# Feed-forward weight sums by accumulating transfers instead of VectorE, with other slots for the token factors

## The chip, the cores and the metric

The kernel runs on one core of a Trainium2 chip. Its time is the device time of one execution in microseconds, and lower is better. A core has TensorE (matrix products into PSUM), VectorE, ScalarE and GpSimd (elementwise work in SBUF, the first two also from PSUM), and SyncE, which here issues most of the DMA transfers. Each engine works through its own queue in order.

## The reference

One inference step of a two-layer decoder trunk for a prompt of 512 tokens and a sample group of 8 x 4 tokens; D_MODEL is 1024. Layer 0 mixes by Mamba-2 SSD heads and sliding-window attention, layer 1 by a forgetting attention over paged caches. Each layer then has cross-attention into 256 memory tokens and a feed-forward part; that part holds most of what is changed:

```python
def swiglu(xn, w_in, w_out):
    g, u = jnp.split(xn @ w_in, 2, axis=-1)
    return (jax.nn.silu(g) * u) @ w_out

for l in range(DEPTH):
    ...  # mixing: layer 0 even_split / ssm / swa, layer 1 odd_split / fox
    xp = xp + cross_attn(rms_norm(xp, norm_xa[l]), mk, mv, w_xq[l], w_xo[l])
    xs = xs + cross_attn(rms_norm(xs, norm_xa[l]), cache_mem_k[l], cache_mem_v[l], w_xq[l], w_xo[l])
    ...
    xp = xp + swiglu(rms_norm(xp, norm_ffn[l]), w_ffn_in[l], w_ffn_out[l])
    xs = xs + swiglu(rms_norm(xs, norm_ffn[l]), w_ffn_in[l], w_ffn_out[l])
```

All 544 tokens (512 prompt, 32 sample) go through the products together. The hidden width is 2816, 22 blocks of 128 for g and u each. All data are float32.

## The kernel before

**Order.** The program is written in one order, but a scheduler places each engine's instructions by a simulated timeline, subject to data dependencies, the number of buffers of each tile, and a few order-only edges (`after`). It also packs the tiles into SBUF by their lifetimes, so a tile may reuse the bytes of one that is done.

**Precision.** A float32 product is made of three passes: each operand is split into a rounded high part (a ScalarE cast) and a remainder (a VectorE subtraction), and TensorE adds high·high, high·low and low·high. So each weight block costs one transfer, one cast and one subtraction before it can be used.

**Slots.** `H` is a pool of 13 equal slots of 128 x 2176 float32. Tokens x (2 slots), their high and low parts (4), hidden blocks, attention tiles and token factors all come from it. `wpiece` streams other weights through `raw` (2 buffers), `wh` and `wl` (3 each).

**The feed-forward stage** (`ffn`, called once per layer). The first 3 of the 22 hidden blocks are computed by `plain`, 8 chunks of 128 deep and three passes each, for g and u, in two halves of the tokens. For the other 19 blocks the product of one 2 x 2 block matrix (weights) by another (tokens) is made with seven products instead of eight. `operands` makes the seven token factors b11, b21, b22, t1 to t4 once per stage: VectorE first writes the normalised tokens `xn` (2 slots of H), GpSimd forms differences and a sum in place (L1424, L1429), and each factor goes into a slot of H as cast and remainder (L1415, L1419, or L1417 when its sign changes). `factors` makes the seven weight factors of a hidden block: SyncE loads `raw` (tag `fr`, two buffers, 1 MB, four quarters; L1440), and `split` writes high and low parts (L1450, L1451) into `fh` and `fl` (three buffers each, two factors in one) or into `f1` (two buffers, a22 alone). The four sums s1 to s4 are formed in place in `raw` by VectorE (L1457, L1458, L1460):

```python
        split(("a11", "a12"), raw[:, 2:4])
        split(("a22",), raw[:, 0:1])
        nc.vector.tensor_tensor(raw[:, 0:2], raw[:, 0:3:2], raw[:, 1:2].to_broadcast([P, 2, 512]), ALU.add)
        nc.vector.tensor_tensor(raw[:, 2], raw[:, 2], raw[:, 0], ALU.add)
        split(("s1", "s2"), raw[:, 0:3:2])
        nc.vector.tensor_tensor(raw[:, 3], raw[:, 3], raw[:, 2], ALU.add)
        split(("s3", "s4"), raw[:, 1:4:2])
```

The seven products (`product`, L1467, 12 matmuls each) of block n are made in the order a11, a12, s1, s2 (`begin`, `second`, `third`), and after the next block's a11 s3, then after its a12 a22 and s4 (`fourth`, `last`). a11, s2, s3 and a22 add up in one PSUM bank R, which is copied out between them (to S0, S1, S2: L1540, L1553, L1557; the last through the SiLU into SG, L1564); s1 and s4 add up in R2. GpSimd then multiplies the two halves of the block (L1569), and the result is split into hidden slots. Between the products, `more` puts pieces of the output projection of a finished group of hidden blocks (`outer`, matmuls at L135, weights by `pair`, L1507 and L1508, evacuation L1520).

**The mixing layers.** `even` and `odd` project tokens to V (with dt or the forget gate) by two weight pieces of 4 x 272 columns from `wpiece`; `stack_q` makes a stacked query tile `QS`; `fox_sample` keeps a small tile `ncs`.

Of the kernel before, what the change touches and what calls it, by code (L numbers as in the profile page):

```python
# [19 lines left out]
P = 128  # L20
# [82 lines left out]
class Net:  # L103
# [37 lines left out]
    def wpiece(self, src, kt, w):  # L141
        nc = self.nc
        n = kt * w
        raw = self.wp.tile([P, 1088], F32, tag="raw", bufs=2, name=self.nm("raw"))
        d = nc.sync.dma_start(raw[:, 0:n], src)
# [5 lines left out]
        nc.scalar.copy(hi[:, 0:n], raw[:, 0:n])  # L151
        nc.vector.tensor_tensor(lo[:, 0:n], raw[:, 0:n], hi[:, 0:n].bitcast(F32), ALU.subtract)  # L152
# [292 lines left out]

    def stack_q(self, pool, q, m, tok):

        nc = self.nc
        Q = pool.tile([P, 1088], F32R, tag="QS", bufs=2, name=self.nm("QS"))[:, 0:1024].rearrange("p (r i t) -> p r i t", r=2, i=4)
        for r in range(2):  # L450
            a, b = slice(64 * r, 64 * r + 64), slice(64 - 64 * r, 128 - 64 * r)
            src = q.half(m)[a, :, tok]
            nc.scalar.copy(Q[a, r], src)
            nc.vector.tensor_tensor(Q[b, r], src, Q[a, r].bitcast(F32), ALU.subtract)
        return Q


    def swa_prompt(self, q, K2, V, m):
        nc = self.nc
        for c in range(4):  # L460
            nk = 1 if c == 0 else 2
            W, k0 = 128 * nk, 128 * max(c - 1, 0)
            tok = slice(128 * c, 128 * c + 128)
            Q = self.stack_q(self.sw, q, m, tok)
            PT = self.H("PT")[:, 0:2048].rearrange("p (k r i t) -> p k r i t", k=2, r=2, i=4)
# [122 lines left out]
    def even(self, st, nxt, fill):  # L588
        nc, tc, I, O = self.nc, self.tc, self.I, self.O
        with ExitStack() as es:  # L590
# [9 lines left out]

            wv = [self.wpiece(I["we_v"][i], 4, 272) for i in range(2)]
            nc.gpsimd.memset(dt, 0.0)
# [359 lines left out]
    def odd(self, st, nxt, fill):  # L962
        nc, tc, I, O = self.nc, self.tc, self.I, self.O
        with ExitStack() as es:
# [52 lines left out]
            with tc.tile_pool(name="fox", bufs=1) as fx:  # L1017
                self.pvs = []
# [18 lines left out]
                smp = self.fox_sample(q, kTs, Qb, V, lf, fx, S, sel)  # L1037
# [12 lines left out]
                for c in range(2):  # L1050
                    o, N = CH[c]
                    for j in range(8):
                        last = self.split(oh, ol, q[j][:, o:o + N], j, o, N)
                self.x_load(self.xd, last)
                self.cross_keys(1, last)
                st2 = nxt()
                self.linear(self.pieces(I["wo_d"], KD), range(8), KD, oh, ol, self.x_evac(st2), tail=2, lead=3)
                self.hold = self.whold = None
        return st2

    def fox_prompt(self, q, K2, V, ncum, oh16, fx, m, c, at=(), smp=None):
        nc = self.nc
        W = 128 * (c + 1)
        tok = slice(128 * c, 128 * c + 128)
        Q = self.stack_q(fx, q, m, tok)
        PT = [self.H("PT")[:, 0:2048].rearrange("p (k r i t) -> p k r i t", k=2, r=2, i=4) for _ in range(c // 2 + 1)]
        for r in range(2):
            for i in range(4):
# [9 lines left out]
                nc.vector.tensor_reduce(nm, sc[:, 0:W], AX.X, ALU.max, negate=True)  # L1078
                pr = fx.tile([P, 512], F32, tag="P", bufs=3, name=self.nm("pr"))
                nc.scalar.activation(pr[:, 0:W], sc[:, 0:W], AF.Exp, bias=nm, accum_out=den)  # L1080
                nc.vector.reciprocal(rec, den)
# [57 lines left out]

    def fox_sample(self, q, kTs, Qb, V, lf, fx, S, sel):  # L1140

        nc, I = self.nc, self.I
        c = self.cst
        ncs = fx.tile([32, 16, 4], F32, name="ncs")
        tp = self.psum("tp", [P, 16])
# [290 lines left out]
    def factors(self, src, fp, prev):  # L1436
# [19 lines left out]

        nc.vector.tensor_tensor(raw[:, 0:2], raw[:, 0:3:2], raw[:, 1:2].to_broadcast([P, 2, 512]), ALU.add)  # L1457
        nc.vector.tensor_tensor(raw[:, 2], raw[:, 2], raw[:, 0], ALU.add)  # L1458
        split(("s1", "s2"), raw[:, 0:3:2])
        nc.vector.tensor_tensor(raw[:, 3], raw[:, 3], raw[:, 2], ALU.add)  # L1460
        split(("s3", "s4"), raw[:, 1:4:2])
# [7 lines left out]
    def ffn(self, l, st, nxt):  # L1469
        nc, tc, I = self.nc, self.tc, self.I  # L1470
        with tc.tile_pool(name=f"ffn{l}", bufs=1) as fp:
            t = fp.tile([P, 10 * HT], F32, name="ft")
            part = lambda a, n: t[:, HT * a:HT * (a + n)]
            U, SG, S0, S1, S2, G1 = (part(0, 2), part(2, 2)), part(4, 2), part(6, 1), part(7, 1), part(8, 1), part(9, 1)
            hh, hl = {}, {}
# [8 lines left out]
            def plain(n):  # L1484
                hidden(n)
                wu, wg = (self.wpiece(I["wfi0"][l, 2 * n + r], KD, 128) for r in range(2))
                for c in (0, 1):
# [7 lines left out]
                    g, s = U[n % 2][:, o:o + N], SG[:, o:o + N]  # L1495
                    nc.vector.tensor_tensor(g, pg[:, 0:N], rb, ALU.mult)  # L1496
# [39 lines left out]
            def begin(n):  # L1536
                w = self.factors(I["wfi1"][l, n - FLEAD], fp, ready if n > FLEAD else gate)
                R = self.psum("tr", [P, HT])
                self.product(R, w["a11"], X["b11"], True)
                nc.scalar.copy(S0, R)  # L1540
                return {"n": n, "w": w, "R": R, "u": U[n % 2]}

            def second(p):
                R3 = self.psum("pv", [P, HT])
                self.product(R3, p["w"]["a12"], X["b21"], True)
                nc.vector.tensor_tensor(p["u"][:, 0:HT], R3, S0, ALU.add)

            def third(p, k):
# [3 lines left out]
                self.product(p["R"], p["w"]["s2"], X["t2"], False)  # L1552
                nc.scalar.copy(S1, p["R"])  # L1553

            def fourth(p):
                self.product(p["R"], p["w"]["s3"], X["t3"], False)
                nc.scalar.copy(S2, p["R"])  # L1557
                nc.vector.tensor_tensor(G1, p["R2"], S2, ALU.add)
                nc.scalar.activation(SG[:, HT:NT], G1, AF.Silu, scale=-1.0)

            def last(p, k):
                n = p["n"]
                self.product(p["R"], p["w"]["a22"], X["t4"], False)
                nc.scalar.activation(SG[:, 0:HT], p["R"], AF.Silu, scale=-1.0)  # L1564
                more(k)
                self.product(p["R2"], p["w"]["s4"], X["b22"], False)
                self.last = nc.vector.tensor_tensor(p["u"][:, HT:NT], p["R2"], S1, ALU.add)  # L1567
                hidden(n)
                nc.gpsimd.tensor_tensor(p["u"], p["u"], SG, ALU.mult)  # L1569
                self.split({n: hh[n][:, n % 4]}, {n: hl[n][:, n % 4]}, p["u"], n, 0, NT)  # L1570
                group(n)
# [167 lines left out]
```

## Time and profile before

| | us |
|---|---|
| median of 3 runs | 1732.09 (1731.93 to 1732.36) |
| the profiled execution's own time | 1733.22 |
| span of the profile | 1731.4 |
| TensorE busy | 1666.6 (96%) |
| VectorE busy | 1200.5 (69%) |
| ScalarE busy | 776.9 (45%) |
| GpSimd busy | 429.4 (25%) |

The profiled execution is one of its own, not one of the three timed runs. PE is TensorE, PEld its weight loads, DVE VectorE, ACT ScalarE, POOL GpSimd, SP SyncE. L1457 is line 1457 of the kernel before. A group's row names line, engine, operation, output <- inputs and shape. Rows of the order in time give start, length, engine, line and operation, and in square brackets how long the engine had been idle and what ended that. Times are from the span's start. TensorE's matmuls overlap, so a matmul of 288 ns follows the one before it after about 126 ns.

### The profile page before, as it was taken

Reading aid. Unit: us, or ns where it says so; the run is one execution under the profiler, and the core shown is the slowest. Engines: PE = TensorE matmul, PEld = TensorE weight load, DVE = VectorE, ACT = ScalarE, POOL = GpSimd, SP = SyncE. Lnnn points to the kernel's source line nnn. Section 1 sums busy time; section 2 is a strip of 40 time slices with the busy share of each in tenths; the row PEclk is TensorE's granted clock in tenths of the full one; section 3 lists DMA queues with packets and bytes.
Section 4 is the critical chain, followed back from the end, with each engine's and each line's share of the span. In section 5 each row is a group of like instructions: output and inputs, shape, how many; then the busy total and the mean of one; then the engine's idle time right before and its main releaser. Section 6 shows DMA issues by size and latency. Waiting matters only on the chain.

```text
span 1731.4 us, 32174 instructions
## 1 busy us (share of the span) xinstructions
PE 1666.6 (96%) x12824; PEld 1531.3 (88%) x12824; DVE 1200.5 (69%) x2142; ACT 776.9 (45%) x1575; POOL 429.4 (25%) x550
## 2 busy tenths in 40 slices
PE   6999999989999989999999999889999899999997
PEld 6988899866997989999999997556898899999997
DVE  6667679867866897777766567335577887777753
ACT  4345435344545454444435345325446354444443
POOL 5022323566422511111113013012222501111112
PEclk9999999989999999999999999899999999999999
DMA  4211423127533142222214423444442142323212
GB/s 157 90 50 50 131 93 129 44 94 253 182 98 135 62 146 86 97 98 86 98 40 135 149 62 113 159 171 151 166 143 91 65 148 92 107 78 110 86 47 80
DMA packets 57106, 189.24 MB, mean 109 GB/s; under 512 B 6044, under 2 KB 16060, under 8 KB 49084
## 3 DMA queue, kind: packets, MB, share of 16 engines
q1 hardware_dynamic: 55268, 184.83, 31.9%
q8 instruction: 101, 1.65, 0.4%
q10 hardware_dynamic: 1608, 1.83, 0.4%
q0 software_dynamic: 80, 0.52, 0.1%
q14 instruction: 49, 0.40, 0.1%
HBM read 172.22 MB, written 14.95 MB: 108 GB/s over the span
## 4 chain that ended last, share of the span: by engine, by line
PE 84%; DVE 7%; DMA 3%; ACT 2%; issue 1%; POOL 1%; SPq 1%; DVEq 0%; ACTq 0%; POOLq 0%
PE ps L135 59%; PE ps L1467 23%; PE ps L138 3%; DMA kv<-fox_kv 1%; DVE wl L152 1%; DMA raw<-we_x 1%; DVE fl L1451 1%; DVE xn L1409 1%; DVE xl L228 1%; SPq L1158 0%; DMA raw<-wfo 0%; POOL ft L1498 0%; DMA hb<-state 0%; DVE fr L1457 0%; DVE xs L853 0%
## 5 line engine op out<-in xcount | busy, mean ns | idle before, releaser
L1467 PE MATMUL ps<-xf,fh 128*128 128x272 f32 x1824 | 355.3, 291 | 11.4 <-DVE ft L1496 3.7
L135 PE MATMUL ps<-xh,wh 128*128 128x288 f32 (+1 forms) x1088 | 319.3, 295 | 8.8 <-ACT wh L151 7.9
L135 PE MATMUL ps<-xl,wh 128*128 128x288 f32 (+1 forms) x1088 | 319.5, 295 | 1.2 <-DVE xl L228 1.0
L135 PE MATMUL ps<-xh,wl 128*128 128x288 f32 (+1 forms) x1088 | 317.9, 293 | 1.9 <-DVE wl L152 1.9
L1467 PEld LDWEIGHTS ps<-xf,fh 128*128 128x128 f32 x1824 | 290.1, 190 | 13.6 <-ACT xf L1415 6.8
L1467 PE MATMUL ps<-xf,fl 128*128 128x272 f32 x912 | 258.2, 292 | 0.0
L135 PEld LDWEIGHTS ps<-xh,wh 128*128 128x128 f32 x1088 | 206.4, 190 | 12.6 <-ACT wh L151 7.9
L135 PEld LDWEIGHTS ps<-xl,wh 128*128 128x128 f32 x1088 | 206.3, 190 | 7.1 <-issue 4.9
L1569 POOL TENSOR_TENSOR ft<-ft 128x544 f32<-128x544 f32 x38 | 78.9, 2076 | 527.7 <-DVE ft L1567 512.7
L135 PEld LDWEIGHTS ps<-xh,wl 128*128 128x128 f32 x1088 | 206.5, 190 | 3.3 <-DVE wl L152 2.2
L151 ACT CAST wh<-raw 128x1024 fp32r<-128x1024 f32 (+2 forms) x128 | 130.9, 1023 | 173.8 <-PE ps L135 98.8
L1451 DVE TENSOR_TENSOR fl<-fr,fh 128x1024 fp32r<-128x1024 f32 x114 | 173.7, 1525 | 23.8 <-ACT fh L1450 23.6
L152 DVE TENSOR_TENSOR wl<-raw,wh 128x1024 fp32r<-128x1024 f32 (+2 forms) x128 | 160.7, 1256 | 30.4 <-ACT wh L151 15.2
L1467 PEld LDWEIGHTS ps<-xf,fl 128*128 128x128 f32 x912 | 170.8, 190 | 0.0
L1450 ACT CAST fh<-fr 128x1024 fp32r<-128x1024 f32 x114 | 119.8, 1053 | 94.0 <-DVE fr L1458 51.8
L135 PE MATMUL ps<-hl,oh 128*128 128x256 f32 (+1 forms) x512 | 147.4, 289 | 0.0
L135 PE MATMUL ps<-hh,ol 128*128 128x256 f32 (+1 forms) x512 | 147.1, 288 | 0.0
L135 PE MATMUL ps<-hh,oh 128*128 128x256 f32 (+1 forms) x512 | 146.2, 288 | 0.0
L237 POOL TENSOR_TENSOR room<-room,sq 128x256 f32<-128x256 f32 (+1 forms) x96 | 84.9, 886 | 184.7 <-ACT sq L236 182.7
L135 PEld LDWEIGHTS ps<-hl,oh 128*128 128x128 f32 x512 | 96.5, 188 | 0.0
L135 PEld LDWEIGHTS ps<-hh,oh 128*128 128x128 f32 x512 | 96.3, 189 | 0.0
L135 PEld LDWEIGHTS ps<-hh,ol 128*128 128x128 f32 x512 | 96.3, 188 | 0.0
(425 smaller groups left out, 3783.6 us busy)
## 6 DMA issues: line engine op xcount, KB each, us to landing
fr<-wfi SPq DMA_DIRECT2D x38, 1024.0 KB
or<-wfo SPq DMA_DIRECT2D x32, 512.0 KB
kv<-fox_kv SPq DMA_DIRECT2D x64, 256.0 KB
raw<-wo_e SPq DMA_DIRECT2D x16, 512.0 KB
xk<-mem_k SPq DMA_DIRECT2D x8, 1024.0 KB
xv<-mem_v SPq DMA_DIRECT2D x8, 1024.0 KB
raw<-we_x SPq DMA_DIRECT2D x12, 512.0 KB
raw<-wfi SPq DMA_DIRECT2D x12, 512.0 KB
```

Of the source, the lines that this page charges most:

```text
L135: self.nc.tensor.matmul(out, lhsT, rhs, start=start, stop=stop)
L138: self.nc.tensor.transpose(out, in_, self.ident[0:k, 0:k])
L151: nc.scalar.copy(hi[:, 0:n], raw[:, 0:n])
L152: nc.vector.tensor_tensor(lo[:, 0:n], raw[:, 0:n], hi[:, 0:n].bitcast(F32), ALU.subtract)
L228: return nc.vector.scalar_tensor_tensor(ll, src, g, hh.bitcast(F32), ALU.mult, ALU.subtract)
L237: nc.gpsimd.tensor_tensor(acc, acc, sq[:, 0:N], ALU.add)
L1409: nc.vector.scalar_tensor_tensor(xn[k], self.x[k], self.par[:, st["g"] + k:st["g"] + k + 1], st["b"], ALU.mult, ALU.mult)
L1450: nc.scalar.copy(hi, t)
L1451: nc.vector.tensor_tensor(lo, t, hi.bitcast(F32), ALU.subtract)
L1467: self.nc.tensor.matmul(ps, w[a][:, k], x[:, b, k], start=start and k == 0 and i == 0, stop=k == 3 and i == 2, skip_group_check=True)
L1569: nc.gpsimd.tensor_tensor(p["u"], p["u"], SG, ALU.mult)
```

## The change

The three VectorE additions that make the weight sums become three transfers issued by GpSimd, which add their source to what stands in the destination. The first reads two quarters of the block from DRAM once more and adds them to the first two quarters in SBUF; the second and third go from SBUF to SBUF. `xn` gets two buffers of its own in the stage's pool instead of two slots of H. The stage's work tile `ft` shrinks from 10 x 272 to 4 x 544 columns: S0, S1, S2 and G1 go, their values stand in the final places U and G, and G has two copies where SG had one. The streaming buffers shrink from 1088 to 1024 columns; the V weights of both mixing layers, which are wider, go through `vpieces` and three slots of H. `QS` shrinks in the same way, and `ncs` moves into an unused part of the tile of `odd`.

```diff
     def wpiece(self, src, kt, w):
...
-        raw = self.wp.tile([P, 1088], F32, tag="raw", bufs=2, name=self.nm("raw"))
+        raw = self.wp.tile([P, 1024], F32, tag="raw", bufs=2, name=self.nm("raw"))
...
-        hi = self.wp.tile([P, 1088], F32R, tag="wh", bufs=3, name=self.nm("wh"))
-        lo = self.wp.tile([P, 1088], F32R, tag="wl", bufs=3, name=self.nm("wl"))
+        hi = self.wp.tile([P, 1024], F32R, tag="wh", bufs=3, name=self.nm("wh"))
+        lo = self.wp.tile([P, 1024], F32R, tag="wl", bufs=3, name=self.nm("wl"))
...
+    def vpieces(self, src):
+
+        nc = self.nc
+        raw, hi, lo = self.H("vr"), self.H("vh", F32R), self.H("vl", F32R)
+        out = []
+        for i in range(2):
+            s = slice(1088 * i, 1088 * i + 1088)
+            nc.sync.dma_start(raw[:, s], src[i])
+            nc.scalar.copy(hi[:, s], raw[:, s])
+            nc.vector.tensor_tensor(lo[:, s], raw[:, s], hi[:, s].bitcast(F32), ALU.subtract)
+            out.append([t[:, s].rearrange("p (k w) -> p k w", w=272) for t in (hi, lo)])
+        return out
...
-            wv = [self.wpiece(I["we_v"][i], 4, 272) for i in range(2)]
+            wv = self.vpieces(I["we_v"])
...
+            ncs = t[0:32, 2016:2080].rearrange("p (h t) -> p h t", h=16)
             xh, xl = st["h"], st["l"]
-            wv = [self.wpiece(I["wd_v"][i], 4, 272) for i in range(2)]
+            wv = self.vpieces(I["wd_v"])
...
     def operands(self, st, fp):
...
         xn = Big(self, "xn")
+        xn.h = [fp.tile([P, 4 * NT], F32, tag="xn", bufs=2, name=self.nm("xn")).rearrange("p (k t) -> p k t", k=4) for _ in range(2)]
...
     def factors(self, src, fp, prev):
...
-        nc.vector.tensor_tensor(raw[:, 0:2], raw[:, 0:3:2], raw[:, 1:2].to_broadcast([P, 2, 512]), ALU.add)
-        nc.vector.tensor_tensor(raw[:, 2], raw[:, 2], raw[:, 0], ALU.add)
+        add = lambda out, in_: nc.gpsimd.dma_start(out, in_, accum_op=ALU.add)
+        add(raw[:, 0:2], src.rearrange("p (a w) -> p a w", a=4)[:, 1:3])
+        add(raw[:, 2], raw[:, 0])
         split(("s1", "s2"), raw[:, 0:3:2])
-        nc.vector.tensor_tensor(raw[:, 3], raw[:, 3], raw[:, 2], ALU.add)
+        add(raw[:, 3], raw[:, 2])
         split(("s3", "s4"), raw[:, 1:4:2])
...
     def ffn(self, l, st, nxt):
...
-            t = fp.tile([P, 10 * HT], F32, name="ft")
-            part = lambda a, n: t[:, HT * a:HT * (a + n)]
-            U, SG, S0, S1, S2, G1 = (part(0, 2), part(2, 2)), part(4, 2), part(6, 1), part(7, 1), part(8, 1), part(9, 1)
+            t = fp.tile([P, 4 * NT], F32, name="ft")
+            U, G = ([t[:, NT * i:NT * i + NT] for i in r] for r in ((0, 1), (2, 3)))
...
-                nc.scalar.copy(S0, R)
-                return {"n": n, "w": w, "R": R, "u": U[n % 2]}
+                nc.scalar.copy(U[n % 2][:, 0:HT], R)
+                return {"n": n, "w": w, "R": R, "u": U[n % 2], "g": G[n % 2]}
...
-                nc.scalar.copy(S2, p["R"])
-                nc.vector.tensor_tensor(G1, p["R2"], S2, ALU.add)
-                nc.scalar.activation(SG[:, HT:NT], G1, AF.Silu, scale=-1.0)
+                g = p["g"][:, HT:NT]
+                nc.scalar.copy(g, p["R"])
+                nc.vector.tensor_tensor(g, p["R2"], g, ALU.add)
+                nc.scalar.activation(g, g, AF.Silu, scale=-1.0)
...
-                self.last = nc.vector.tensor_tensor(p["u"][:, HT:NT], p["R2"], S1, ALU.add)
+                self.last = nc.vector.tensor_tensor(p["u"][:, HT:NT], p["R2"], p["u"][:, HT:NT], ALU.add)
                 hidden(n)
-                nc.gpsimd.tensor_tensor(p["u"], p["u"], SG, ALU.mult)
+                nc.gpsimd.tensor_tensor(p["u"], p["u"], p["g"], ALU.mult)
```

More of the change, by code (lines that the diff above doesn't have):

```diff
@@ L444, in stack_k, with stack_q @@
         return kh, kl
-    def stack_q(self, pool, q, m, tok):
+    def stack_q(self, Q, q, m, tok):
         nc = self.nc
-        Q = pool.tile([P, 1088], F32R, tag="QS", bufs=2, name=self.nm("QS"))[:, 0:1024].rearrange("p (r i t) -> p r i t", r=2, i=4)
+        Q = Q.rearrange("p (r i t) -> p r i t", r=2, i=4)
         for r in range(2):
@@ L463, in swa_prompt @@
             tok = slice(128 * c, 128 * c + 128)
-            Q = self.stack_q(self.sw, q, m, tok)
+            Q = self.stack_q(self.sw.tile([P, 1024], F32R, tag="QS", bufs=2, name=self.nm("QS")), q, m, tok)
             PT = self.H("PT")[:, 0:2048].rearrange("p (k r i t) -> p k r i t", k=2, r=2, i=4)
@@ L1017, in odd @@
             with tc.tile_pool(name="fox", bufs=1) as fx:
-                self.pvs = []
+                self.pvs, self.heads = [], 0
                 K2 = self.stack_k(kT)
@@ L1036, in odd @@
                 next(f)
-                smp = self.fox_sample(q, kTs, Qb, V, lf, fx, S, sel)
+                smp = self.fox_sample(q, kTs, Qb, ncs, V, lf, fx, S, sel)
                 heads = 0
@@ L1064, in fox_prompt @@
         tok = slice(128 * c, 128 * c + 128)
-        Q = self.stack_q(fx, q, m, tok)
+        Q = self.stack_q(fx.tile([P, 1024], F32R, tag="QS", bufs=2, name=self.nm("QS"))[:, 0:1024], q, m, tok)
         PT = [self.H("PT")[:, 0:2048].rearrange("p (k r i t) -> p k r i t", k=2, r=2, i=4) for _ in range(c // 2 + 1)]
@@ L1138, in fox_bias, with fox_sample @@
         return S, sel.rearrange("p a t -> p (a t)")
-    def fox_sample(self, q, kTs, Qb, V, lf, fx, S, sel):
+    def fox_sample(self, q, kTs, Qb, ncs, V, lf, fx, S, sel):
         nc, I = self.nc, self.I
         c = self.cst
-        ncs = fx.tile([32, 16, 4], F32, name="ncs")
         tp = self.psum("tp", [P, 16])
@@ L1545, in second @@
                 self.product(R3, p["w"]["a12"], X["b21"], True)
-                nc.vector.tensor_tensor(p["u"][:, 0:HT], R3, S0, ALU.add)
+                nc.vector.tensor_tensor(p["u"][:, 0:HT], R3, p["u"][:, 0:HT], ALU.add)
             def third(p, k):
```

7 lines of the change are left out of this document (4 added, 3 removed).

## The prediction

> **What bounds the kernel now.** I read the table of busy time first, then windows, then the chain that ended last for single stretches, then the order in time of VectorE, ScalarE and GpSimd there.
>
> ```profile
> span 1731.4 us, 32174 instructions
> PE 1666.6 (96%) x12824; PEld 1531.3 (88%) x12824; DVE 1200.5 (69%) x2142; ACT 776.9 (45%) x1575; POOL 429.4 (25%) x550
> 600.00:650.00 50.00, 44.74 (x328) 43.86 (x327) 46.42 (x54) 24.69 (x37) 13.87 (x6) 0.93 0.36 127
> 640.00:890.00 250.00, 250.00 (x1989) 250.00 (x1989) 183.88 (x242) 106.26 (x164) 32.90 (x15) 1.00 0.27 91
> 1350.00:1400.00 50.00, 44.92 (x336) 44.01 (x335) 48.42 (x52) 24.60 (x36) 22.20 (x10) 0.93 0.27 105
> 1400.00:1650.00 250.00, 250.00 (x1989) 250.00 (x1988) 185.44 (x242) 106.31 (x165) 32.34 (x16) 1.00 0.29 96
> ```
>
> A window row gives its length, then busy time of TensorE, weight loads, VectorE, ScalarE and GpSimd, the granted clock, the DMA share and GB/s. The two long rows are the feed-forward stages, where all that the title names happens: TensorE is busy 250.00 of 250 us at clock 1.00. VectorE has 183.88 of 250, so 26% of its time is free, and time taken from it there is worth nothing by itself. The two short rows are the starts of these stages. TensorE stands still for 5.26 and 5.08 us, and VectorE is nearly full (46.42 and 48.42 of 50). Only these 10.3 us are to be won in the feed-forward stages.
>
> **The sums.** In before they are three VectorE instructions per hidden block:
>
> ```profile
> L1457 DVE TENSOR_TENSOR fr<-fr x38: 1212/1216/3200, 604.1 to 1664.3; 128x1024 f32<-128x1024 f32 x38
> L1458 DVE TENSOR_TENSOR fr<-fr x38: 677/679/1521, 607.6 to 1667.8; 128x512 f32<-128x512 f32 x38
> L1460 DVE TENSOR_TENSOR fr<-fr x38: 675/679/694, 608.5 to 1669.1; 128x512 f32<-128x512 f32 x38
> ```
>
> By the medians 38 x (1.216 + 0.679 + 0.679) = 97.8 us leave VectorE. In the full stretches this is nothing on the path. In exchange come 38 x 3 transfers on GpSimd's queue of 512, 256 and 256 KB, in series: the second reads what the first wrote, the third what the second wrote. So the question is how late the weights s1 may be. One block in the steady stretch, by the chain (start, length, what), then VectorE, ScalarE, GpSimd, and one row of TensorE a block later:
>
> ```profile
> 658.48 4.54 PE ps L1467 x36
> 671.40 1.51 PE ps L1467 x12
> 675.10 4.54 PE ps L1467 x36
> 661.84 0.69 DVE L1451 TENSOR_TENSOR f<-fr,f 128x512 fp32r<-128x512 f32 x1 [1.16 <-ACT f L1450]
> 669.08 1.22 DVE L1451 TENSOR_TENSOR fl<-fr,fh 128x1024 fp32r<-128x1024 f32 x1 [0.23 <-ACT fh L1450]
> 671.62 1.23 DVE L1451 TENSOR_TENSOR fl<-fr,fh 128x1024 fp32r<-128x1024 f32 x1 [0.49 <-ACT fh L1450]
> 660.90 0.40 ACT L1564 ACTIVATE ft<-ps 128x272 f32<-128x272 f32 x1 [1.48 <-PE ps L1467]
> 661.20 0.61 ACT L1450 CAST f<-fr 128x512 fp32r<-128x512 f32 x1
> 667.99 1.06 ACT L1450 CAST fh<-fr 128x1024 fp32r<-128x1024 f32 x1 [2.08 <-DVE fr L1458]
> 668.95 0.37 ACT L1553 COPY ft<-ps 128x272 f32<-128x272 f32 x1
> 663.05 2.17 POOL L1569 TENSOR_TENSOR ft<-ft 128x544 f32<-128x544 f32 x1 [13.79 <-DVE ft L1567]
> 692.45 1.68 PE L1467 MATMUL ps<-xf,f 128*128 128x272 f32 x12
> ```
>
> A block lasts 675.10 - 658.48 = 16.62 us. The first transfer overwrites the quarter that the split of a22 reads, so it can start when that split ends, 661.84 + 0.69 = 662.53. The split itself starts as soon as TensorE lets go of a22 two blocks back (660.90), since f1 has two buffers, so this point can't move forward. The other end: after s3 (12 matmuls from 671.40) and a run of the output projection comes a group of 36 from 675.10. A block later the a22 product (the row with f) starts 0.7 us after the group's start (691.7), so some matmuls of s1 or of s4 stand ahead of it. If s1 is first in the group, it is wanted at 675.10; if last, at 679.64 - 1.51 = 678.1. Before it stand the ScalarE cast and VectorE's remainder, 1.06 + 1.22 = 2.3 us. So the first two transfers have 675.1 - 2.3 - 662.5 = 10.3 us, or 13.3.
>
> What do they take? No accumulating transfer stands in before. The nearest rows:
>
> ```profile
> L1103 POOL DMA_INDIRECT lg<-fox_logf,pg x1: 1134/1134/1134, 984.0 to 984.0; - x1
> L1101 ACTq DMA_DIRECT2D pg<-page_col x1: 529/529/529, 980.0 to 980.0; - x1
>   DMA pg<-page_col: 3.4, 1
> DMA to landing us min/median/max: 6.2/6.2/6.2
> q0 software_dynamic: 80, 0.52, 0.1%
> 579.08 0.33 SPq L145 DMA_DIRECT2D raw<-wfi  x1
> 582.68 1.05 ACT L151 CAST wh<-raw 128x1024 fp32r<-128x1024 f32 x1 [1.89 <-DMA raw<-wfi]
> ```
>
> The gather of 0.52 MB is the only transfer that GpSimd issues; it holds that engine 1.13 us and lands after 6.2. A plain load of 512 KB from SyncE's queue goes from issue (579.08) to use (582.68) in 3.6. One of 64 numbers, issued by ScalarE, kept GpSimd waiting 3.4. For the first transfer (512 KB) the ends are 3.6 and 12.4 (the gather twice, since an addition reads both operands); I take 6.2, the row with its size and queue. For the second and third (256 KB) the ends are 3.4 and 6.2; I take 5.1, halfway between the 4.0 of that smallest one (from its issue at 980.0 to 984.0) and 6.2. The first two: 11.3 (ends 7.0 and 18.6).
>
> The Trainium skill, DMA: Bandwidth & Descriptors, section "Anatomy of one DMA — SWDGE (gpsimd) path", gives 2.0 us plus bytes over 436 GB/s. By that, as an estimate, they would take 3.2 and 2.6, together 5.8, and be hidden at either place of s1; the 6.2 of the gather, against 3.2 by that rule, speaks for more.
>
> There is one more thing on GpSimd's queue: the product L1569, 663.05 to 665.22. If it goes ahead of the first transfer, this is issued 2.7 us later. So four corners, missing us per block: s1 first and GpSimd free 11.3 - 10.3 = 1.0; s1 first and behind L1569 3.7; s1 last and free none; s1 last and behind 11.3 + 2.7 - 13.3 = 0.7. The order is made anew by the scheduler, so I take the lower of the two middle corners, 0.7, for (19 - 2) x 2 = 34 steady blocks: **+24 us**. Missing time isn't made up, since TensorE has no free time in a block.
>
> Behind the waiting instructions: on ScalarE the cast for s1 and s2 stands just ahead of L1553, which must empty a bank before s3 adds to it at 671.40. If the cast stays there, its room is 671.4 - 0.4 - 1.1 - 662.5 = 7.4 us, not 10.3 (a rival below). On GpSimd L1569 may wait for a landing, and behind it the split of the hidden block; this is hidden unless a group of hidden blocks ends. The third transfer and the splits of s3 and s4: 662.5 + 11.3 + 0.7 + 5.1 + 2.3 = 681.9, wanted a block after 671.40, at 688.0: hidden by 6 us. The load buffer comes free then, 9 us later than now (671.62 + 1.23); its next load is wanted two blocks after 661.20, at 694.4, and 1 MB at twice 3.6 us lands at 689: hidden by 5. Transfers grow by 38 MB on 189; the share of 0.27 to 0.29 stays far from 1, but the later load now falls beside the next first transfer (upper end).
>
> **The start of each stage.** The token factors:
>
> ```profile
> 597.30 3.56 DVE L1451 TENSOR_TENSOR fl<-fr,fh 128x1024 fp32r<-128x1024 f32 x1
> 600.78 3.05 DVE L1451 TENSOR_TENSOR f<-fr,f 128x512 fp32r<-128x512 f32 x1
> 604.12 3.20 DVE L1457 TENSOR_TENSOR fr<-fr 128x1024 f32<-128x1024 f32 x1
> 609.41 2.89 DVE L1451 TENSOR_TENSOR fl<-fr,fh 128x1024 fp32r<-128x1024 f32 x2 [0.19 <-ACT fh L1450]
> 612.93 1.28 DVE L1419 TENSOR_TENSOR xf<-xn,xf 128x1088 fp32r<-128x1088 f32 x1
> 610.53 2.11 ACT L1415 ACTIVATE xf<-xn 128x1088 fp32r<-128x1088 f32 x2
> 603.36 2.88 POOL L1424 TENSOR_TENSOR xn<-xn,xn 128x1088 f32<-128x1088 f32 x1
> PE ps L1467 <- ACT xf L1415: 2.6, 1, 2.6
> PE ps L1467 <- DVE xf L1419: 2.2, 1, 2.2
> PE ps L1467 <- DVE ft L1496: 3.7, 1, 3.7
> ```
>
> TensorE waits 4.8 us for t1, whose cast starts at 610.53 although GpSimd's differences are done at 606.24: t1 needs one of 13 slots H, all taken until the last plain block lets go of its tokens. Taking xn out of H gives two slots sooner, and the sums' 3.20 + 2 x 0.68 = 4.6 us leave VectorE, for whose late evacuation L1496 the second stage waits 3.7 us. That alone would take away the whole stall, 10.3 us over both stages. But here the split of a22 ends at 603.83, the weights s1 then follow 11.3 + 2.3 us later, at 617.4, or at 613.9 if that split goes ahead of the 3.56 us one; t1's wait ended at 612.93 + 1.28 = 614.2. One stall takes the other's place: I take 0, between -5.2 (a whole stall of a stage gone) and +3.2 (617.4) for each.
>
> **The rest**, each at nothing. Buffers of 1024 instead of 1088, ncs inside another tile, and U and G in place of S0, S1, S2, SG: the same instructions and sizes, and in the long stretches TensorE waits for none of these tiles (250.00 of 250). In both mixing layers V's weights take three H slots instead of the streaming buffers: the same loads, casts and remainders. Their bounds:
>
> ```profile
> PE ps L135 <- ACT wh L151: 8.3, 3, 7.9
> PE ps L135 <- DVE wl L152: 1.9, 1, 1.9
> ```
>
> An earlier load could save the 1.9; two 544 KB loads ahead of others at the kernel's beginning could cost two times 3.6. I keep 0.
>
> **Sum.** 24 + 0 + 0 on the profiled execution, 1733.2 (span 1731.4 and 1.8 around it), gives 1757; the median of the runs is 1.1 lower, so **1756**.
>
> **Rivals.** *Hidden after all* (faster): the first two transfers take under 10.3 us with s1 first, or under 13.3 with s1 last, so no steady block waits, and the starts lose part or all of 10.3 us: 1722 to 1728. For it: both middle corners miss by at most 1.0, and TensorE has fillers to put ahead. It decides at one number, the landing of the second transfer at 672.8 in the block shown. The skill's rule above would lead here. Chance 0.33. *It does nothing*: hidden, and the start's stall only changes its name: within 0.2% (3.5 us, about what a measurement of this kernel can tell from no change). Chance 0.13. *Far dearer*: the cast holds up L1553 (11.3 - 7.4 = 3.9 us per block, 34 x 3.9 = 133, 1864), or the transfers take their upper 18.6 us (8.3 x 34 = 282, 2013). Against the second: the DMA share is low (0.27); for it: an addition has two operands to read. Chance 0.10. The skill, Collectives: The Full Stack, section "The bandwidth ceiling: the fold count and why AG ≠ RS ≠ AR", states that an add in the DMA engines halves the rate through its two source reads; no run so far shows it here. *The forecast*, 0.1 to 2 us missing per steady block: 1736 to 1800, chance 0.44.
>
> The range reaches from the faster rival's 1722 to 1803 (2 us per block and 3 per start over the forecast's base); it leaves out the far dearer case and a little beside it. The forecast's own range is 1736 to 1800. Faster 0.33, same 0.13, slower 0.44 + 0.10 = 0.54.
>
> **What would show it.** Right: windows in the long stretches with TensorE under 250 of 250 and VectorE down by 2.6 us per block; ScalarE's cast for s1 and s2 waiting for a transfer into fr; TensorE waiting for fh there; 11 us from the split of a22 to the second landing. The start: t1's cast before 606, and a wait for fh in its place. Wrong: 250.00 of 250 again (hidden), or a wait for a copy of the banks, L1553 (the dearer case).

## The result, and the profile after

The changed kernel takes 1896.43 us (median of 4 runs, 1888.76 to 1903.93), against 1732.01 (1730.58 to 1732.36): a ratio of 1.0951, 95% interval 1.0901 to 1.1. That is 164.4 us slower, 140 above the forecast and beyond the range. The profiled execution took 1888.76. From its page (busy time, a DMA queue with packets, MB and share, and two groups of transfers with their median landing):

```profile
span 1887.0 us, 32221 instructions
PE 1721.2 (91%) x12824; PEld 1575.7 (84%) x12824; DVE 1096.6 (58%) x2028; ACT 768.0 (41%) x1575; POOL 512.0 (27%) x664
...
q0 software_dynamic: 16496, 40.38, 12.5%
...
fr<-wfi POOLq DMA_DIRECT2D x38, 512.0 KB, 6.8
fr<-fr POOLq DMA_DIRECT2D x76, 256.0 KB, 3.3
```

VectorE lost 103.9 us of work. The first transfer lands a little later than the prediction sized it, the second and third sooner: 6.8 and 3.3 us against 6.2 and 5.1. The windows of the two starts and the two long stretches:

```profile
600.00:650.00 50.00, 37.18 (x240) 35.57 (x239) 32.83 (x31) 18.09 (x28) 19.34 (x14) 0.83 0.50 134
640.00:890.00 250.00, 221.81 (x1598) 218.62 (x1599) 118.35 (x163) 88.01 (x139) 52.95 (x51) 0.91 0.54 132
1440.00:1490.00 50.00, 40.87 (x290) 39.56 (x290) 38.31 (x38) 20.26 (x31) 22.91 (x14) 0.93 0.45 116
1490.00:1740.00 250.00, 217.96 (x1617) 215.41 (x1616) 113.72 (x162) 85.46 (x136) 55.70 (x50) 0.94 0.54 133
```

TensorE starts 1598 matmuls in 250 us where before it started 1989. Measured from the first matmul of `product` to the last, a feed-forward stage takes 383.8 and 378.0 us, against 310.3 and 309.7. That is 141.8 of the 155.6 us by which the span grew; 4.6 lie ahead of the first stage, 8.5 between the stages, 0.7 behind. A block takes 19.8 us (mean distance of its first transfers) in place of 16.62. Who waits (us in total, times, longest):

```profile
PE ps L1483 <- ACT ft L1573: 65.7, 25, 5.6
PE ps L1483 <- ACT fh L1465: 27.1, 12, 5.4
PE ps L1483 <- DVE fl L1466: 8.7, 5, 3.1
ACT fh L1465 <- DMA fr<-fr: 264.5, 73, 7.9
POOL fr L1472 <- DVE f L1466: 288.5, 38, 9.7
```

L1483 is the product, L1465 and L1466 the split, L1472 the transfers, L1573 the copy S2, L1580 the SiLU behind a22. TensorE waits mostly for a small copy, S2, and that copy is late because ScalarE stands in front of it waiting for a transfer: in 29 of the 38 blocks S2's copy starts directly behind a cast that has waited for one. The chain of work over two rounds, then ScalarE's order in the first of them:

```profile
726.73 6.31 DMA fr<-wfi
...
733.58 3.30 DMA fr<-fr
...
736.95 1.05 ACT fh L1465
...
740.77 1.52 PE ps L1483 x12
...
742.32 0.40 ACT ft L1580
742.72 0.52 ACT f L1465
...
743.26 0.70 DVE f L1466
...
744.24 8.78 DMA fr<-wfi
...
757.13 3.27 DMA fr<-fr
...
760.43 1.04 ACT fh L1465
761.47 0.29 ACT ft L1573
...
766.86 5.92 DMA fr<-wfi
```

```profile
736.95 1.04 ACT L1465 CAST fh<-fr 128x1024 fp32r<-128x1024 f32 x1 [3.44 <-DMA fr<-fr]
737.90 0.38 ACT L1573 COPY ft<-ps 128x272 f32<-128x272 f32 x1
740.50 1.05 ACT L1465 CAST fh<-fr 128x1024 fp32r<-128x1024 f32 x1 [2.23 <-DMA fr<-fr]
...
742.32 0.40 ACT L1580 ACTIVATE ft<-ps 128x272 f32<-128x272 f32 x1 [0.43 <-PE ps L1483]
742.61 0.61 ACT L1465 CAST f<-fr 128x512 fp32r<-128x512 f32 x1
```

The chain bites its own tail. The split of a22 releases the first transfer (744.24); the transfers release the cast of s1 and s2, or that of s3 and s4; behind this cast on ScalarE stands S2's copy of the block before; this copy releases TensorE's a22 product; that product lets go of one of the two buffers of `f1`, and so the next a22 split (742.72) can run and releases the next first transfer. From 726.73 to 744.24 the loop takes 17.5 us (the first and second transfer in it), from 744.24 to the next first transfer, at 766.86, 22.6 (all three). Before, the same loop held 2.6 us of VectorE's sums and had slack; now it holds 10 to 16 us of landings and is longer than the 16.6 us that TensorE needs for a block.

### The profile page after: what moved, and what is told of

It is laid out like the page before. It is cut to its first block, busy times and chain, and to the rows that moved or that the text cites. A ratio compares the mean times of both kernels' runs of the same rounds, so it can differ in the third digit from the quotient of the medians.

```text
span 1887.0 us, 32221 instructions
## 1 busy us (share of the span) xinstructions
PE 1721.2 (91%) x12824; PEld 1575.7 (84%) x12824; DVE 1096.6 (58%) x2028; ACT 768.0 (41%) x1575; POOL 512.0 (27%) x664
## 3 DMA queue, kind: packets, MB, share of 16 engines
q0 software_dynamic: 16496, 40.38, 12.5%
## 4 chain that ended last, share of the span: by engine, by line
PE 50%; DMA 22%; issue 10%; DVE 9%; ACT 5%; POOL 3%; SPq 1%; DVEq 0%; POOLq 0%; ACTq 0%
PE ps L135 42%; DMA fr<-wfi 12%; DMA fr<-fr 6%; PE ps L1483 5%; PE ps L138 3%; ACT fh L1465 2%; POOL fr L1472 1%; DVE f L1466 1%; DVE xl L241 1%; DMA kv<-fox_kv 1%; DVE wl L152 1%; DVE fl L1466 1%; POOL room L412 1%; DMA raw<-we_x 1%; SPq L1172 1%
## 5 line engine op out<-in xcount | busy, mean ns | idle before, releaser
L1483 PE MATMUL ps<-xf,fh 128*128 128x272 f32 x1824 | 370.6, 301 | 31.9 <-ACT fh L1465 27.1
L1483 PEld LDWEIGHTS ps<-xf,fh 128*128 128x128 f32 x1824 | 306.0, 201 | 35.5 <-ACT fh L1465 29.9
L1466 DVE TENSOR_TENSOR fl<-fr,fh 128x1024 fp32r<-128x1024 f32 x114 | 160.8, 1413 | 287.4 <-ACT fh L1465 287.4
L1483 PE MATMUL ps<-xf,fl 128*128 128x272 f32 x912 | 270.6, 299 | 8.7 <-DVE fl L1466 8.7
L1465 ACT CAST fh<-fr 128x1024 fp32r<-128x1024 f32 x114 | 119.1, 1048 | 276.6 <-DMA fr<-fr 264.5
L1483 PEld LDWEIGHTS ps<-xf,fl 128*128 128x128 f32 x912 | 180.1, 199 | 10.0 <-DVE fl L1466 10.0
L151 ACT CAST wh<-raw 128x1024 fp32r<-128x1024 f32 (+1 forms) x124 | 126.0, 1019 | 130.9 <-PE ps L135 83.1
L152 DVE TENSOR_TENSOR wl<-raw,wh 128x1024 fp32r<-128x1024 f32 (+1 forms) x124 | 157.0, 1267 | 25.4 <-PE ps L135 17.5
L1483 PE MATMUL ps<-xf,f 128*128 128x272 f32 x456 | 87.3, 356 | 65.7 <-ACT ft L1573 65.7
L1472 POOL DMA_DIRECT2D fr<-fr x76 | 66.3, 872 | 275.6 <-DMA fr<-wfi 150.0
L1483 PEld LDWEIGHTS ps<-xf,f 128*128 128x128 f32 x456 | 78.9, 247 | 71.6 <-ACT ft L1573 71.6
L1472 POOL DMA_DIRECT2D fr<-wfi x38 | 33.2, 875 | 288.5 <-DVE f L1466 288.5
```

What stands on the lines that cost most here:

```text
L1465: nc.scalar.copy(hi, t)
L1466: nc.vector.tensor_tensor(lo, t, hi.bitcast(F32), ALU.subtract)
L1472: add = lambda out, in_: nc.gpsimd.dma_start(out, in_, accum_op=ALU.add)
L1483: self.nc.tensor.matmul(ps, w[a][:, k], x[:, b, k], start=start and k == 0 and i == 0, stop=k == 3 and i == 2, skip_group_check=True)
```

## The experiments

Each kernel's time is beside a kernel before on the same chip (medians 1730.9 to 1732.0). A stage length is, as above, the time from the first to the last matmul of `product`.

**The slots alone.** VectorE's three sums put back into the changed kernel:

```diff
-        add = lambda out, in_: nc.gpsimd.dma_start(out, in_, accum_op=ALU.add)
-        add(raw[:, 0:2], src.rearrange("p (a w) -> p a w", a=4)[:, 1:3])
-        add(raw[:, 2], raw[:, 0])
+        nc.vector.tensor_tensor(raw[:, 0:2], raw[:, 0:3:2], raw[:, 1:2].to_broadcast([P, 2, 512]), ALU.add)
+        nc.vector.tensor_tensor(raw[:, 2], raw[:, 2], raw[:, 0], ALU.add)
...
-        add(raw[:, 3], raw[:, 2])
+        nc.vector.tensor_tensor(raw[:, 3], raw[:, 3], raw[:, 2], ALU.add)
```

> All of the change but the transfers: the sums are VectorE additions again, the slots are the new ones. Theory A (the whole loss is a loop through ScalarE's queue: a22's split, the three transfers, the casts of s1/s2 and s3/s4, which stand in that queue ahead of the copy S2, then S2, a22, and the next split): no loss is left, 1722 to 1735, below 1732 only if the stall at the start of the feed-forward stages (10.3 us) shrinks. Rival S (the new slots and the packing of SBUF cost much of it): 1760 or more.

1745.7 us, ratio 1.0075 (1.0061 to 1.0089): 14 us slower, between the two expectations, stages 312.1 and 311.8, and in a long stretch TensorE is full again:

```profile
1420.00:1670.00 250.00, 250.00 (x1989) 250.00 (x1988) 180.48 (x241) 103.01 (x164) 32.66 (x15) 1.00 0.26 88
```

**The transfers alone.** The four `add` lines in the kernel before, with its slots.

> Only the accumulating transfers on the kernel before, old slots. Theory A: as slow as the whole change or within 15 us of it, 1880 to 1910, with ScalarE waiting for transfers into fr and TensorE waiting for the copy S2. Rival S: well below 1880.

1877.94 us, ratio 1.0840 (1.0823 to 1.0858): 146.6 us slower, 2 us short of the first theory's 1880, stages 386.9 and 383.2. TensorE's longest wait is again the one for S2's copy (74.9 us in total). 14 and 147 make 161 of the 164: the two halves add up, and nine tenths are the transfers.

**A third buffer for a22's split** (`tag="f1", bufs=3`), all transfers kept.

> The changed kernel with a third buffer for f1, so a22's split may run a block earlier and the first transfer no longer waits for the last a22 product. Theory A: the loop is cut at that link, 1735 to 1790. Rival B (the loss is the added DMA traffic, 40 MB, slowing loads and engines): still 1880 to 1900. Rival L (the first transfers are simply longer than the room before s1): little changes, over 1850.

1844.22 us, ratio 1.0652 (1.0634 to 1.0671): 52 us of the 164 back. All three expectations are missed: it is 54 us above the first theory's upper end and 6 to 36 us below its rivals'. Stages 358.4 and 353.5. Here the loop is cut at one place, with every byte still moved. It closes anew through the loaded block, whose two buffers are let go of only by the split of s3 and s4 (below, a load starts at 770.30 as that split ends, and the next a22 split waits for it), and S2's copy still stands behind a cast that waits. From the chain:

```profile
767.97 1.05 ACT fh L1465
...
770.30 6.06 DMA fr<-wfi
...
776.43 0.62 ACT f L1465
...
785.14 3.27 DMA fr<-fr
...
788.49 1.04 ACT fh L1465
789.53 0.29 ACT ft L1573
```

**Another order.** Two buffers, but both casts of a block's sums stand behind the S2 copy of the block before (an order-only edge, `self.after`, on the first cast; the third transfer and the second cast are written behind it).

> The changed kernel with one order-only edge per block: the casts of s1/s2 and s3/s4 go behind the copy S2 of the block before on ScalarE. Transfers, bytes and buffers are the same. Theory A: TensorE no longer waits for S2; but the SiLU after a22 and the next split of a22 now stand behind both casts, so a shorter loop is left, 0.6 + 0.7 + 6.8 + 3.3 + 3.3 + 1.1 + 1.0 + 0.4 = 17.2 us and some issue time against 16.6 per block: 1755 to 1820. Rivals B and L: 1870 to 1900.

1882.16 us, ratio 1.0876 (1.0851 to 1.0901): only 14 us back. The first theory's 1755 to 1820 is missed, and the time lies where both rivals, the bytes and the transfers too long for their room, had put it; taken alone this run speaks for them. Its waits say more. The one for S2's copy (L1578 here) is nearly gone, 0.9 us in place of 65.7, but TensorE now waits for the casts themselves, and the loop closes elsewhere: the remainder of a22's split stands on VectorE behind that of s3 and s4 (L1468 here, the first transfer is L1474):

```profile
PE ps L1488 <- ACT fh L1465: 37.1, 28, 3.8
PE ps L1488 <- DVE fl L1468: 36.2, 42, 3.1
...
PE ps L1488 <- ACT ft L1578: 0.9, 2, 0.5
```

```profile
746.04 3.28 DMA fr<-fr
...
749.34 1.06 ACT fh L1465
...
752.01 0.61 DVE f L1468
...
752.91 8.62 DMA fr<-wfi
```

So to name one waiting row and move it isn't enough. Which of the loop's ends TensorE waits for is a matter of order; its length is what counts. Whether bytes, or the transfers' length by itself, could make the loss is decided by the runs below.

**One part of the sums by transfer.** First the first sum only, then the second and third only; VectorE makes the others.

```diff
 # first only
         add(raw[:, 0:2], src.rearrange("p (a w) -> p a w", a=4)[:, 1:3])
-        add(raw[:, 2], raw[:, 0])
+        nc.vector.tensor_tensor(raw[:, 2], raw[:, 2], raw[:, 0], ALU.add)
...
-        add(raw[:, 3], raw[:, 2])
+        nc.vector.tensor_tensor(raw[:, 3], raw[:, 3], raw[:, 2], ALU.add)
 # second and third only
-        add(raw[:, 0:2], src.rearrange("p (a w) -> p a w", a=4)[:, 1:3])
+        nc.vector.tensor_tensor(raw[:, 0:2], raw[:, 0:3:2], raw[:, 1:2].to_broadcast([P, 2, 512]), ALU.add)
         add(raw[:, 2], raw[:, 0])
...
         add(raw[:, 3], raw[:, 2])
```

> The changed kernel with only the first sum (s1 and half of s2, 512 KB from DRAM) by an accumulating transfer; the other two sums are VectorE's again. Loop theory: a block of the changed kernel takes 19.8 us because three transfers stand one after another (6.84 + 3.36 + 3.36 by their own landings, and two casts of about 0.7) in a loop that closes through the two buffers of a22's split, so all else in the loop is 19.8 - 14.4 or about 5.4 us. With one transfer and two additions of VectorE the loop is 5.4 + 6.84 + 0.7 + 0.7, 13.7 us, shorter than the 16.6 us that TensorE needs for a block: the loss of the transfers goes nearly whole and the time is that of the slots alone, 1745 (1740 to 1760). Rival, the bytes of the added transfers hold up the loads and TensorE's data: this one moves half of the added 1 MB of a block, so half of the 147 us of loss stays, about 1820. Rival, a fixed price for each transfer (GpSimd's 0.87 us and its start): a third of the loss stays, about 1795.

> The complement: the first sum by VectorE, the second and third by transfers of 256 KB each from SBUF. Loop theory: the loop is 5.4 + 1.2 + 2 x 3.36 + 0.8, 14.1 us, below TensorE's 16.6: about 1745, at most 1765, since it lies nearer to the bound. Rival of the bytes: half of the loss stays, about 1820. Rival of a fixed price for each transfer: two thirds stay, about 1845.

1763.99 us, ratio 1.0187 (1.0160 to 1.0214), and 1769.53, ratio 1.0212 (1.0188 to 1.0237). Stages 315.6 and 316.1, and 323.1 and 324.1. Above the slots' 1745.7 these are 18 and 24 us, 42 together, where both at once cost 151. Bytes or a price for each transfer would add up; a loop that becomes the bound only when it passes 16.6 us does not. Both came out above the loop theory's 1745, by 19 and 24 us, and just above the ranges given with it (1760 and 1765). In the first, 12 us of this stand in layer 1's mixing, between the stages (469.5 us against 457.5 with the slots alone), where the program is the same and only the scheduler's order differs.

**Plain transfers**: `accum_op` left out.

> The changed kernel with plain transfers in place of the accumulating ones (nothing is added, so s1 to s4 are not the sums; the order, sizes and waits are the same). If the addition itself makes a transfer long, the landings fall below 6.8 and 3.3 us, and by the loop theory the time falls by 34 x 1.0 us for each microsecond that the three lose together (a first transfer of 5.5 would give about 1850). If the length is that of issue and of moving the bytes, landings and time stay, 1880 to 1905.

1775.38 us in one run; stages 320.8 and 324.7.

```profile
q0 software_dynamic: 11632, 40.38, 6.5%
...
fr<-wfi POOLq DMA_DIRECT2D x38, 512.0 KB, 4.8
fr<-fr POOLq DMA_DIRECT2D x76, 256.0 KB, 2.3
```

The same bytes in the same order and with the same waits, but 4.0 us less in the three medians of a block together (9.4 against 13.4; by the means 3.5): the loop falls to 19.8 - 4.0 = 15.8, or to 16.3, under TensorE's 16.6, and 121 us go. By itself this doesn't tell the landings from the DMA engines' time, since their share falls too, from 12.5% to 6.5%; the next two runs do.

**Links without bytes.** The slots with VectorE's sums, and behind each sum one or two transfers of 1 KB of the sum onto itself (the second of the three sums shown):

```diff
         nc.vector.tensor_tensor(raw[:, 2], raw[:, 2], raw[:, 0], ALU.add)
+        nc.gpsimd.dma_start(raw[0:16, 2, 0:16], raw[0:16, 2, 0:16])
+        nc.gpsimd.dma_start(raw[0:16, 2, 0:16], raw[0:16, 2, 0:16])   # only with six in a block
```

> The slots with VectorE's sums, and behind each sum one transfer of 1 KB (16 partitions x 64 bytes of the sum copied onto themselves), so that all that needs the sum waits for a transfer, but hardly a byte is moved. Loop theory: the loop is 5.4 + 2.6 (VectorE's sums) + three landings; a 1 KB landing isn't shown yet, an estimate is 1.5 to 2.2 us (256 KB of plain copy took 2.3), so 12.5 to 14.6 us: below 16.6, and the time is that of the slots and a little, 1745 to 1770. Rival of the bytes and of the DMA engines' time: 1745, since nothing is moved.

> The same with two 1 KB transfers one behind the other after each sum, six in a block. Loop theory: 5.4 + 2.6 + 6 x (1.5 to 2.2) = 17 to 21.2 us a block, above TensorE's 16.6: the time rises by 34 x 0.4 to 4.6 over the kernel with three, 1765 to 1910, and the landings measured in it say where in this. Rival of the bytes and of the DMA engines' time: 1745 as with three, at most 1755.

With three 1763.31 us, ratio 1.0184 (1.0153 to 1.0214); with six 1820.34, ratio 1.0521 (1.0488 to 1.0553). Queue, landing and the first long stretch, three links first:

```profile
q0 software_dynamic: 3728, 0.65, 0.3%
...
fr<-fr POOLq DMA_DIRECT2D x114, 1.0 KB, 1.6
```

```profile
640.00:940.00 300.00, 297.35 (x2352) 295.96 (x2352) 210.05 (x283) 125.27 (x205) 66.44 (x72) 1.00 0.27 91
```

```profile
q0 software_dynamic: 7376, 0.77, 0.3%
...
fr<-fr POOLq DMA_DIRECT2D x228, 1.0 KB, 1.5
```

```profile
640.00:940.00 300.00, 282.36 (x2167) 279.37 (x2167) 191.12 (x265) 115.18 (x184) 82.03 (x120) 0.97 0.25 83
```

With 0.12 MB more, and a DMA share no higher than before, the second three links cost 57 us, three times what the first three cost over the slots (18). In the two stages alone, where the links are, it is 62 against 11; the rest lies in layer 1's mixing, 9 us longer with three links than with six. This is the theory's sharpest case, and the rival of the bytes (1745 to 1755) falls. TensorE waits here for the casts themselves (27.0 us) and hardly for S2's copy (0.4): serial links cost time although this loop doesn't close through that copy; where it closes wasn't worked out. Its sizes were off: with the mean landing of 2.08 us, six links would make 5.4 + 2.6 + 12.5 = 20.5 us a block, but toward the end of a stage a block takes 17.5 (mean of the last 14 distances between casts of a22). So the 5.4 us for the rest of the loop, taken from a mean over blocks of two kinds, was too high by about 3 for this kernel. A part of that is a slip in the sum behind it: its terms make 15.0, not 14.4, and leave 4.8.

**Three buffers of both kinds.** All three accumulating transfers, with three buffers for `f1` and for the loaded block, the output weights' split reduced to one each to make room; then the same with the order of the fourth experiment.

```diff
-        raw = fp.tile([P, 4, 512], F32, tag="fr", bufs=2, name=self.nm("fr"))
+        raw = fp.tile([P, 4, 512], F32, tag="fr", bufs=3, name=self.nm("fr"))
...
-                one = fp.tile([P, 2, 512], F32R, tag="f1", bufs=2, name=self.nm("f1"))
+                one = fp.tile([P, 2, 512], F32R, tag="f1", bufs=3, name=self.nm("f1"))
...
-                hi, lo = (fp.tile([P, 1024], F32R, tag=g, bufs=2, name=self.nm(g)) for g in ("oh", "ol"))
+                hi, lo = (fp.tile([P, 1024], F32R, tag=g, bufs=1, name=self.nm(g)) for g in ("oh", "ol"))
```

> The changed kernel, all three accumulating transfers kept, with three buffers for a22's split and three for the loaded blocks (the tiles of the output weights' split have one buffer instead of two, which gives the memory). Loop theory: with a third buffer of both kinds the loop closes over three blocks instead of two, the transfers of one block run beside the products of another, and the time falls below the 1844 of the three split buffers alone, to 1760 to 1810 (GpSimd's queue still takes the transfers one after another, 5.9 + 3.4 + 3.4 and its other work, near 16.6). Rival of the bytes and of the DMA engines' time: the same bytes are moved and the time stays at 1840 or above.

> All three accumulating transfers, three buffers of both kinds, and also the order of the fourth experiment: both casts of a block's sums behind S2's copy of the block before. With three buffers 1814 was measured and a block still took 17.7 to 18.3 us, against TensorE's 16.6. If what is left is that casts which wait for a transfer stand ahead of the copies and SiLUs that TensorE and the next a22 split need, this order removes it now that the buffers give room: 1750 to 1790. If it is GpSimd's queue, where the three transfers stand one behind another with the product between them (6.9 + 4.4 + 4.4 and 2.2 us, 17.9 a block), the order changes nothing: 1800 to 1825. If the split of a22, which stands behind SiLU on ScalarE whatever buffers there are, is pushed later by casts that wait, it gets slower: above 1825.

1813.58 us, ratio 1.0485 (1.0449 to 1.0521), just above the upper end expected; and 1789.42, ratio 1.0346 (1.0314 to 1.0378), just inside the first theory's. Stages 343.2 and 334.7, then 327.1 and 330.6. The second of the two, second long stretch and queue:

```profile
1420.00:1670.00 250.00, 240.61 (x1854) 237.56 (x1854) 126.37 (x185) 99.49 (x159) 63.54 (x59) 0.98 0.64 162
```

```profile
q0 software_dynamic: 16496, 40.38, 12.6%
```

All 40.38 MB are moved, the DMA share is higher (0.64 against 0.54), and the landings are longer (7.5 and 4.6 us on the mean against 6.8 and 3.4), yet 107 of the 164 us are back. So neither bytes nor DMA time, nor the length of the transfers by itself, make most of the loss. The order that gave 14 us with two buffers gave 24 with three: TensorE's waits for the copies of S1 and S2, 15.7 and 4.5 us with three buffers alone, are gone but for 0.9. The expectation from GpSimd's queue (the order changes nothing, 1800 to 1825) falls with it. What is left is 58 us over the kernel before. In the profile 38 of 56 us lie in the stages, where a block still takes 17.2 to 17.3 us late in the stage, and 12 in layer 1's mixing. Why the block isn't at 16.6, and what the single buffers of the output weights cost, wasn't measured. No version beats the kernel before, in which VectorE has these 98 us to spare.

**A part of the slots.** VectorE's sums, and only the slots in the feed-forward stages; V's weights and the 1088 columns as before.

> The slots alone (sums by VectorE), and of these only the part in the feed-forward stages (token factors' own slots, the smaller tile of products, the bias of fox_sample inside another tile); the value weights' pieces stay as before, in the rows of 1088. The slots together cost 14 us: of it about 8 came up between 430 and 470 us, ahead of the first feed-forward stage, and 2.3 at the start of each feed-forward stage. If the jump is from the value pieces and the shorter slots of the weights, it goes here: 1731 + 5, about 1736. If the jump is the scheduler's order of layer 0, made anew whatever slot is changed, it stays or comes out at random: 1740 to 1750.

1740.09 us, ratio 1.0048 (1.0029 to 1.0066), at the lower end of what the scheduler's order was expected to give. In the profiles, aligned by the count of matmuls, the slots alone lose 6 us between 420 and 474 (a load of layer 0's output weights that the chain waits for ends at 445.6 instead of 430.9); this kernel doesn't, but loses 3.7 by 256 us, which the other doesn't. Both lose about 2 at the start of each feed-forward stage (2.3 and 2.5; 2.3 and 1.3). So the starts' loss comes with the feed-forward slots, and the rest moves about with the scheduler's order; which slot moves it stays open.

## Why the prediction was wrong

**The sizes of the transfers were not the error.** First and second were put at 11.3 us together. From the issue of the first to the landing of the second it is 10.7 us on the mean: the landings take 6.84 and 3.36, and 0.54 pass between the first landing and the second issue, for which the prediction had no term. By the prediction's own corner (10.3 us of room, s1 first) 0.4 us would be missing per block, less than the 0.7 it took.

**The step that failed: the room was measured from a point that was held fixed.** "The split itself starts as soon as TensorE lets go of a22 two blocks back, so this point can't move forward" is right, but the point can move back, and the landings push it. The prediction had all the pieces (two buffers of f1, the SiLU that ends ahead of the split, casts standing ahead of a bank's copy) and priced them as an open line with 0.7 us missing per block. Closed into a loop, the missing time per block was 3.2 us on the mean (19.8 - 16.6); over the 36 distances from block to block that is 115 of the 141.8 us that the stages lost.

**The third transfer, "hidden by 6 us", is in the loop.** Its cast was said to be wanted only by s3, a block later. But on ScalarE it stands ahead of S2's copy in one kind of block (757.13, 760.43, 761.47 above) and ahead of the SiLU in the other (740.50, 742.32; there it holds nothing up, since the SiLU waits for TensorE). What counted was not who needs its result, but what is queued behind it.

**"The order is made anew by the scheduler"** was used to take a low middle corner. It was made anew: S1's copy (L1568), which the dear rival saw held up, went ahead of the cast, and TensorE waits 0.9 us for it. But both casts stayed ahead of S2's copy or of the SiLU of L1580, which no corner held. That rival, "the cast holds up L1553", priced at 3.9 us per block and 1864, had the right kind of wait at the neighbouring copy, without the loop, and a chance of 0.10. It is the case that came nearest, in part by luck: the copy that it named costs 0.9 us.

**"Missing time" was counted at one for one.** In 640 to 890 us, 31.7 us of the loss are pauses between matmuls (distances over 0.3 us, less the usual 0.126), and another 16 are some 160 matmuls at about 227 ns from start to start, nearly all in stretches with a granted clock of 0.5 after a pause:

```profile
756.00:760.00 4.00, 1.94 (x15) 1.70 (x14) 1.57 (x2) 1.33 (x2) 0.86 (x1) 1.00 0.48 82
760.00:764.00 4.00, 2.19 (x9) 2.19 (x10) 2.27 (x4) 2.22 (x4) 0.00 (x0) 0.53 0.19 27
764.00:768.00 4.00, 4.00 (x22) 4.00 (x22) 2.36 (x3) 2.03 (x4) 0.87 (x1) 0.61 0.85 344
768.00:772.00 4.00, 4.00 (x34) 4.00 (x33) 3.04 (x3) 1.05 (x2) 1.35 (x1) 1.00 0.84 156
```

A pause of 4.2 us (757.65 to 761.81) is followed by 5 us at a clock near 0.5: one more half of the pauses on top of them.

**What held.** VectorE's time left it as said (103.9 us with the changed tiles, 97.8 for the sums) and was worth nothing. One stall did take the other's place at the starts: TensorE waits 6.1 us for s1's high part and remainder in the first stage, and 6.0 in the second (1.6 of it still for the late evacuation), where it waited 4.8 and 4.6 before. By these waits a start lost 1.3 to 1.4 us, within the -5.2 to +3.2 given for each. With the slots alone a start lost 2.3 and 2.5 us, so taking `xn` out of H won nothing. The rest of the slots, kept at 0, cost about 10 us by the medians (4 in the profiled execution), somewhere in the order of the two layers' mixing. One sum has a slip: 2 us per block and 3 for each of two starts make 1806 for the upper end, not 1803, which changes nothing here.

## What to carry to other kernels

Before giving work of an idle engine to transfers, follow the chain past the consumer until it comes back to the producer: through buffer counts, and through what stands behind each waiting instruction on its queue. Add up the whole round and compare it with the bound's time per block; under it the transfers cost little here (8 to 23 us in the two stages), and over it what is too long is paid in every block. A small copy or activation behind a cast that waits for a landing is the first place to look, and one more buffer helps only until the loop closes at the next place.

## What the runs showed of the hardware

An accumulating transfer lands later than a plain one of the same size: 6.8 against 4.8 us for 512 KB from DRAM, 3.3 against 2.3 for 256 KB within SBUF. It holds GpSimd longer (0.87 against 0.55 us), makes more packets (16496 against 11632) and takes about twice the DMA time (12.5% of 1887 us against 6.5% of 1774, or 236 against 115 us). The last agrees with what the Trainium skill, Collectives: The Full Stack, section "The bandwidth ceiling: the fold count and why AG ≠ RS ≠ AR", says of an add's two source reads. By the rule of the Trainium skill, DMA: Bandwidth & Descriptors, section "Anatomy of one DMA — SWDGE (gpsimd) path", the estimates are 3.2 and 2.6 us. The plain ones measure 4.8 and 2.3, the accumulating ones 6.8 and 3.3. A transfer of 1 KB lands in 1.5 to 1.6 by the median.

In the two stages of the changed kernel every one of 12 pauses of TensorE above 3.5 us was followed by a stretch at a granted clock of 0.5, 3.4 or 6.8 us long, with mostly 10 to 24 matmuls at 226 to 227 ns from start to start. So were 12 of 15 pauses between 2.0 and 3.4 us (one more fell inside such a stretch), and none of nine between 1.0 and 1.8. Of the three that were not (2.02, 2.46 and 2.60 us) two are longer than some that were (2.07 and 2.15), so here the length alone didn't decide it. The Trainium skill, TensorE: Matmul & The Clock Gate, section "Part 1: The HAM clock gate (the "warmup" mystery)", describes such a half rate after an idle window of some 3.4 us; the half agrees, and here pauses of 2.1 us were sometimes enough.
